# Last piece of the down projection as two 256-column halves in banks of their own, its sum of squares on DVE, final scaling split 384 to 640

## The chip, the cores and the metric

The kernel runs on one core of a Trainium2 chip. The metric is the device time in microseconds (us). The engines are TensorE (PE, with its weight load PEld), VectorE (DVE), ScalarE (ACT), GpSimd (POOL) and SyncE (SP), which issues most of the DMA.

## The reference, cut to what matters

Two layers, each with an attention mixer and a gated MLP with a causal depthwise convolution, both with a norm in front and a residual add behind; at the end one more RMS norm. The sequence has 256 positions, the model 1024 columns, the MLP 2816.

```python
def rmsnorm(x, g):
    xf = x.astype(jnp.float32)
    y = xf * lax.rsqrt(jnp.mean(xf * xf, axis=-1, keepdims=True) + NORM_EPS)
    return (y * g.astype(jnp.float32)).astype(x.dtype)

def conv_glu_ffn(h, w_up, conv_w, conv_b, w_down):
    a, u = jnp.split(h @ w_up, 2, axis=-1)
    a = lax.conv_general_dilated(...) + conv_b
    return (jax.nn.silu(a) * u) @ w_down

    for i in range(DEPTH):
        ...
        h = rmsnorm(x, norm2_g[i])
        x = x + conv_glu_ffn(h, w_up[i], conv_w[i], conv_b[i], w_down[i])
    return rmsnorm(x, final_g)
```

## The kernel before, in words

The residual stream stays on the chip as `xr`, 128 partitions by two tiles of positions (t = 0, 1) by 1024 columns. fp32 products are made of three matmuls each (`mm3`, L206 to L208: high by high, high by low, low by high), so each weight tile `st` that arrives by DMA is split into a high part `hl` on ACT (L158) and a low part on DVE (L160).

The MLP of a layer goes over NF = 11 blocks of 256 hidden columns. `up(f)` makes 256-column matmuls (L919 to L921) into two banks of role u0 or u1, by f odd or even, then the convolution and the gate on DVE and ACT, and ends in `h_hi` and `h_lo`. `down(fs, which)` adds the down projection of the blocks fs into the banks `dn[n, t]`, where n is the half of 512 output columns and t the tile of positions; in the traces these four banks are called bn. Within the loop, `down` of block f - 1 follows `up(f)` on TensorE. The last two blocks (9 and 10) come after the loop. In the last layer they come piece by piece, in the order (n, t) = (0, 0), (1, 0), (0, 1), (1, 1), 12 matmuls of 512 columns a piece. Behind each piece, `add` (L962) puts the bank and `xr` together on DVE, `sumsq` (L179) squares the 512 columns with a running sum on ACT, and the gain `fg` is multiplied in on POOL for n = 0 and on DVE for n = 1 (L1000).

When both pieces of a tile are there, the mean is put together by POOL (m0, L1002) and DVE (m1, L1003), POOL raises it to the power of -1/2 (L1004), ACT scales the first 512 columns (L1005) and DVE the other 512 (L1007), and the two halves are stored from SP's queue (L1006) and ACT's (L1008). Nothing else is left to do behind the piece (1, 1) of the last layer.

The order of instructions on each engine is made by a scheduler within the framework; each engine runs its own list in order. [...]

## Time and profile before

| | |
|---|---|
| three runs | 661.97, 664.06, 664.2 us; median 664.06 |
| the profiled execution | 662.68 us, span 660.9 us |
| mean granted TensorE clock | 0.997 of full speed |
| busy | PE 97%, PEld 88%, DVE 75%, ACT 57%, POOL 8% |
| chain that ended last | PE 81%, DVE 11%, the rest 2% or less each |

The span runs from the first to the last instruction of the profiled execution; its time is 1.78 us more. A share of busy time is a mean over the whole span. The chain is followed back from the last instruction, at each step to what released it.

### The profile page before, as it was taken

How to read it: one execution, taken by the hardware profiler on the slowest of the kernel's cores; microseconds unless marked ns; L12 is line 12 of the kernel's file. 1: busy time of each engine (PE TensorE's matmuls, PEld its weight loads, DVE VectorE, ACT ScalarE, POOL GpSimd, SP SyncE). 2: the span in 40 equal slices, each digit the busy share in tenths (PEclk: the TensorE clock that was granted, in tenths of full speed). 3: DMA queues.
4: the chain of work that ended last, by engine and by line, in shares of the span. 5: the costliest groups of instructions: out<-in, count | busy, mean ns of one | idle time of the engine just before them, and what ended most of it. 6: DMA issues, size and time to landing. Idle time of an engine off the chain costs nothing.

```text
span 660.9 us, 11729 instructions
## 1 busy us (share of the span) xinstructions
PE 641.7 (97%) x4403; PEld 578.4 (88%) x4403; DVE 497.5 (75%) x1093; ACT 375.5 (57%) x683; POOL 50.3 (8%) x119
## 2 busy tenths in 40 slices
PE   8989999999999999999999999999999999999995
PEld 6978987779999999999898888877999999999994
DVE  5979998776766677777587799986697776666653
ACT  6666667775544444455475676785654455544523
POOL 0522210001000000000020242000000000000002
PEclk9999999999999999999999999999999999999998
DMA  8982423454665565565457525234465655566601
GB/s 268 279 265 72 126 83 113 134 184 158 192 188 185 179 188 184 182 182 160 128 167 228 149 71 176 81 110 155 127 218 189 184 182 182 187 191 190 191 1 63
DMA packets 76535, 107.34 MB, mean 162 GB/s; under 512 B 3717, under 2 KB 63414, under 8 KB 76480
## 3 DMA queue, kind: packets, MB, share of 16 engines
q1 hardware_dynamic: 75568, 104.77, 51.2%
q0 software_dynamic: 448, 1.05, 0.5%
q8 instruction: 34, 0.56, 0.3%
q10 hardware_dynamic: 464, 0.79, 0.3%
q14 instruction: 21, 0.17, 0.1%
HBM read 105.55 MB, written 1.05 MB: 161 GB/s over the span
## 4 chain that ended last, share of the span: by engine, by line
PE 81%; DVE 11%; DMA 2%; issue 2%; ACT 2%; POOL 1%; POOLq 0%; DVEq 0%; ACTq 0%
PE bu L921 13%; PE bu L920 13%; PE bu L919 13%; PE bn L206 6%; PE bn L207 6%; PE bn L208 6%; PE bd L206 5%; PE bd L208 5%; PE bd L207 5%; DVE hl L160 3%; PE bs L352 2%; DMA st<-in_w_in_dram 2%; PE bt L372 2%; PE bt L341 1%; DVE acc L484 1%
## 5 line engine op out<-in xcount | busy, mean ns | idle before, releaser
L160 DVE TENSOR_TENSOR hl<-st,hl 128x1024 fp32r<-128x1024 f32 (+3 forms) x208 | 230.7, 1120 | 97.3 <-ACT hl L158 96.8
L158 ACT CAST hl<-st 128x1024 fp32r<-128x1024 f32 (+3 forms) x208 | 198.0, 970 | 136.4 <-PE bu L921 68.1
L920 PE MATMUL bu<-alo,hl 128*128 128x256 f32 x704 | 199.7, 284 | 1.3 <-DVE alo L196 1.3
L921 PE MATMUL bu<-ahi,hl 128*128 128x256 f32 x704 | 199.0, 283 | 0.0
L919 PE MATMUL bu<-ahi,hl 128*128 128x256 f32 x704 | 197.9, 283 | 0.0
L920 PEld LDWEIGHTS bu<-alo,hl 128*128 128x128 f32 x704 | 135.1, 192 | 2.4 <-DVE alo L196 1.7
L919 PEld LDWEIGHTS bu<-ahi,hl 128*128 128x128 f32 x704 | 134.5, 192 | 1.3 <-ACT ahi L195 0.3
L921 PEld LDWEIGHTS bu<-ahi,hl 128*128 128x128 f32 x704 | 135.1, 192 | 0.0
L206 PE MATMUL bd<-hl,ahi 128*128 128x384 f32 (+2 forms) x256 | 92.9, 367 | 2.3 <-ACT hl L158 1.4
L207 PE MATMUL bd<-hl,ahi 128*128 128x384 f32 (+2 forms) x256 | 91.4, 357 | 0.4 <-DVE hl L160 0.4
L208 PE MATMUL bd<-hl,alo 128*128 128x384 f32 (+2 forms) x256 | 91.2, 356 | 0.0
L206 PE MATMUL bn<-hl,h_hi 128*128 128x512 f32 x176 | 68.9, 392 | 0.0
L207 PE MATMUL bn<-hl,h_hi 128*128 128x512 f32 x176 | 68.6, 391 | 0.0
L208 PE MATMUL bn<-hl,h_lo 128*128 128x512 f32 x176 | 68.4, 390 | 0.0
L206 PEld LDWEIGHTS bd<-hl,ahi 128*128 128x128 f32 x256 | 48.0, 188 | 11.0 <-ACT hl L158 3.0
L207 PEld LDWEIGHTS bd<-hl,ahi 128*128 128x128 f32 x256 | 48.2, 188 | 3.6 <-issue 0.8
L208 PEld LDWEIGHTS bd<-hl,alo 128*128 128x128 f32 x256 | 48.2, 188 | 3.1 <-issue 0.9
L208 PEld LDWEIGHTS bn<-hl,h_lo 128*128 128x128 f32 x176 | 33.0, 188 | 7.4 <-DVE h_lo L943 0.4
L206 PEld LDWEIGHTS bn<-hl,h_hi 128*128 128x128 f32 x176 | 33.1, 188 | 6.6 <-ACT h_hi L942 0.5
L207 PEld LDWEIGHTS bn<-hl,h_hi 128*128 128x128 f32 x176 | 33.1, 188 | 6.0
L931 DVE SCALAR_TENSOR_TENSOR c<-a,colc,c 128x255 f32<-128x255 f32 (+1 forms) x88 | 36.7, 477 | 0.7 <-ACT c L929 0.7
L934 ACT ACTIVATE th<-c 128x512 f32<-128x512 f32 x22 | 13.9, 632 | 35.1 <-DVE c L931 35.1
(242 smaller groups left out, 782.0 us busy)
## 6 DMA issues: line engine op xcount, KB each, us to landing
st<-in_w_up_dram SPq DMA_DIRECT2D x88, 512.0 KB, 3.6
st<-in_w_down_dram SPq DMA_DIRECT2D x44, 512.0 KB, 3.5
st<-in_w_in_dram SPq DMA_DIRECT2D x40, 384.0 KB, 3.8
st<-in_w_out_dram SPq DMA_DIRECT2D x12, 512.0 KB, 3.8
st<-in_w_in_dram SPq DMA_DIRECT2D x8, 360.0 KB, 3.5
st<-in_w_in_dram SPq DMA_DIRECT2D x8, 336.0 KB, 3.6
st<-in_w_out_dram SPq DMA_DIRECT2D x8, 256.0 KB, 3.0
xr<-in_x_dram SPq DMA_DIRECT2D x3, 256.0 KB, 5.9
```

The costliest lines, as they stand in the source:

```text
L158: S.copy(hv, sv)
L160: V.tensor_sub(lv, sv, hv.bitcast(F32))
L206: PE.matmul(b, ahi, whi, start=first, stop=False)
L207: PE.matmul(b, ahi, wlo, start=False, stop=False)
L208: return PE.matmul(b, alo, whi, start=False, stop=last)
L352: PE.matmul(b[:, o:o + nk], qa, ka, start=True, stop=True)
L372: PE.transpose(b[:, j * 128:(j + 1) * 128], P[:, j * 128:(j + 1) * 128], ident)
L919: PE.matmul(o, wa, hhi[k // 4][:, k % 4, :], start=k == 0, stop=False)
L920: PE.matmul(o, wa, hlo[k // 4][:, k % 4, :], start=False, stop=False)
L921: PE.matmul(o, wl, hhi[k // 4][:, k % 4, :], start=False, stop=k == 7)
L931: V.scalar_tensor_tensor(c[:, o + d:o + 256], a[:, o:o + 256 - d], cw[w], c[:, o + d:o + 256], op0=OP.mult, op1=OP.add)
L934: S.activation(th, c, AF.Tanh, scale=0.5)
```

## The change

In the last layer alone:

- The piece (1, 1) of the last two blocks no longer adds into its old bank. That bank's sum ends with block 8 (`f1 = NF - 3`), and `add(1, 1)` takes it into `xr` ahead of the closing loop. The last two blocks make two pieces of 256 columns, each in a bank of role u1 of its own, so the last 12 matmuls of 512 columns become 24 of 256.
- Behind each piece comes an add, a square with a sum into a column of its own, and the gain. For the very last piece the square runs on DVE with an accumulator output (L1011); the others stay on ACT.
- The gain of each tile's last piece is issued on DVE behind the mean instruction (L1017) instead of ahead of it.
- ACT scales 384 columns and DVE 640, and the stores are divided in the same way.

```diff
+                    f1 = NF - 3 if i == DEPTH - 1 and (n, t) == (1, 1) and into is None else NF - 1
...
-                            q, c = slice(t * 128, (t + 1) * 128), slice(n * 512, (n + 1) * 512)
-                            mm3(dn[n, t], h_hi[:, s, q], h_lo[:, s, q], wh[:, 0, c], wl[:, 0, c],
-                                f == 0 and s == 0, f == NF - 1 and s == 1)
+                            q, c = slice(t * 128, (t + 1) * 128), slice(n * 512 + part.start, n * 512 + part.stop)
+                            mm3(dn[n, t] if into is None else into, h_hi[:, s, q], h_lo[:, s, q], wh[:, 0, c], wl[:, 0, c],
+                                f == (0 if into is None else fs[0]) and s == 0, f == f1 and s == 1)
...
+            add(1, 1)
+
             for t in range(2):
-                m0, m1, r = (keep.tile([128, 1], F32, name=f"fin{j}{t}") for j in range(3))
-                y = [mp.tile([128, 512], F32, name=f"y{n}", tag=f"y{n}", bufs=2) for n in range(2)]
-                for n in range(2):
-                    down(fs, [(n, t)])
-                    xs = add(n, t)
-                    sumsq(ssq, t, n)
-                    (V if n else G).tensor_mul(y[n], xs, fg[:, n * 512:(n + 1) * 512])
-                    if n == 0:
-                        G.tensor_scalar(m0, ssq[:, t, 0:1], 1.0 / D, EPS, op0=OP.mult, op1=OP.add)
-                V.scalar_tensor_tensor(m1, ssq[:, t, 1:2], 1.0 / D, m0, op0=OP.mult, op1=OP.add)
-                G.tensor_tensor(r, m1, neghalf[:, 0:1], op=OP.pow)
-                S.activation(y[0], y[0], AF.Copy, scale=r)
-                nc.sync.dma_start(out[0, t * 128:(t + 1) * 128, 0:512], y[0])
-                V.tensor_scalar(y[1], y[1], r, None, op0=OP.mult)
-                nc.scalar.dma_start(out[0, t * 128:(t + 1) * 128, 512:1024], y[1])
+                m = [keep.tile([128, 1], F32, name=f"fin{j}{t}") for j in range(3)]
+                sq = keep.tile([128, 3], F32, name=f"fins{t}")
+                r = keep.tile([128, 1], F32, name=f"finr{t}")
+                y = mp.tile([128, D], F32, name="y", tag="y", bufs=2)
+                pieces = [(0, 0, 512), (1, 0, 512)] if t == 0 else [(0, 0, 512), (1, 0, 256), (1, 256, 512)]
+                for j, (n, a, b) in enumerate(pieces):
+                    last = j == len(pieces) - 1
+                    o = None if b - a == 512 else bank("u1")[:, :b - a]
+                    down(fs, [(n, t)], slice(a, b), o)
+                    xs = add(n, t, slice(a, b), o)
...
+                    if last and t:
+                        V.scalar_tensor_tensor(junk[:, :b - a], xs, 1.0, xs, op0=OP.mult, op1=OP.mult,
+                                               accum_out=sq[:, j:j + 1])
+                    else:
+                        S.activation(junk[:, :b - a], xs, AF.Square, accum_out=sq[:, j:j + 1])
+                    mj = None
+                    if j:
+                        mj = V.scalar_tensor_tensor(m[j], sq[:, j:j + 1], 1.0 / D, m[j - 1], op0=OP.mult, op1=OP.add)
+                    else:
+                        G.tensor_scalar(m[0], sq[:, 0:1], 1.0 / D, EPS, op0=OP.mult, op1=OP.add)
+                    with after(mj.ins if last else None):
+                        (V if j else G).tensor_mul(y[:, c], xs, fg[:, c])
+                G.tensor_tensor(r, m[len(pieces) - 1], neghalf[:, 0:1], op=OP.pow)
+                S.activation(y[:, 0:384], y[:, 0:384], AF.Copy, scale=r)
+                nc.sync.dma_start(out[0, t * 128:(t + 1) * 128, 0:384], y[:, 0:384])
+                V.tensor_scalar(y[:, 384:D], y[:, 384:D], r, None, op0=OP.mult)
+                nc.scalar.dma_start(out[0, t * 128:(t + 1) * 128, 384:D], y[:, 384:D])
```

Three places show what the scheduler makes of it. The first is TensorE's list where the last piece begins, in the changed kernel (the bank of the piece ahead is bn_5469, that of the first half bu_7377):

```order
L208 MATMUL bn_5469<-hl,h_lo 128x512
L206 MATMUL bu_7377<-hl,h_hi 128x256 [waits PE_49]
L207 MATMUL bu_7377<-hl,h_hi 128x256
L208 MATMUL bu_7377<-hl,h_lo 128x256
L206 MATMUL bu_7377<-hl,h_hi 128x256
```

Before, the 12 matmuls that follow bn_5469 write bn_5471 with 512 columns and wait for nothing; now 12 write bu_7377 and 12 more bu_7395, and the first of each has a wait for a count of TensorE itself, one reached when the matmuls of `up(9)` into the same bank were done.

The second place is DVE's list for tile 1, from the add of piece (0, 1) on; fg is the gain, ssq and fins hold the sums of squares, fin is the mean or the power. Before:

```order
L962 TENSOR_TENSOR xr<-bn_5469,xr 128x512 [waits PE_49]
L962 TENSOR_TENSOR xr<-bn_5471,xr 128x512 [waits PE_49]
L1000 TENSOR_TENSOR y_7356<-xr,fg 128x512 [waits DVE_49]
L1003 SCALAR_TENSOR_TENSOR fin_7353<-ssq,fin_7352 128x1 [waits Activation_49,Pool_49]
L1007 TENSOR_SCALAR y_7356<-y_7356,fin_7354 128x512 [waits Pool_49]
```

And in the changed kernel (L964 is the add, L1021 the gain, L1017 the mean, L1011 the square, L1025 the scaling; finr is the power):

```order
L964 TENSOR_TENSOR xr<-bn_5469,xr 128x512 [waits PE_49]
L964 TENSOR_TENSOR xr<-bu_7377,xr 128x256 [waits PE_49]
L1021 TENSOR_TENSOR y<-xr,fg 128x256 [waits DVE_49]
L1017 SCALAR_TENSOR_TENSOR fin_7355<-fins_7357,fin_7354 128x1 [waits Activation_49,Pool_49]
L964 TENSOR_TENSOR xr<-bu_7395,xr 128x256 [waits PE_49]
L1011 SCALAR_TENSOR_TENSOR junk,fins_7357<-xr 128x256 [waits DVE_49]
L1017 SCALAR_TENSOR_TENSOR fin_7356<-fins_7357,fin_7355 128x1 [waits DVE_49]
L1021 TENSOR_TENSOR y<-xr,fg 128x256
L1025 TENSOR_SCALAR y<-y,finr_7358 128x640 [waits DVE_49,Pool_49]
```

Three instructions became two sets for the halves, with a square between the last add and the last mean, and the gain went behind the mean.

The third place is DVE's list between the gate of block 9 (h_lo) and the first vector instruction of block 10 (a), in the changed kernel; hl are the low parts of the last two down weights:

```order
L160 TENSOR_TENSOR hl<-st,hl 128x1024 [waits DMAHW0_49,Activation_49]
L943 TENSOR_TENSOR h_lo<-u,h_hi 128x512 [waits Activation_49]
L964 TENSOR_TENSOR xr<-bn_5471,xr 128x512 [waits PE_49]
L160 TENSOR_TENSOR hl<-st,hl 128x1024 [waits DMAHW1_49,Activation_49]
L160 TENSOR_TENSOR hl<-st,hl 128x1024 [waits DMAHW2_49,Activation_49]
L923 TENSOR_TENSOR a<-bu_7188,R 128x512 [waits PE_49]
```

The add of bn_5471 is new there; before, the two weight splits follow h_lo at once.

## Rows read from the trace of the kernel before

Times of a timeline are the start and the duration in us; "idle before" is how long the engine had waited and for whom.

**Rows 1.** The page: the span, busy time, share and instructions of the engines, and the shares of the chain that ended last.

```profile
span 660.9 us, 11729 instructions
...
PE 641.7 (97%) x4403; PEld 578.4 (88%) x4403; DVE 497.5 (75%) x1093; ACT 375.5 (57%) x683; POOL 50.3 (8%) x119
...
PE 81%; DVE 11%; DMA 2%; issue 2%; ACT 2%; POOL 1%; POOLq 0%; DVEq 0%; ACTq 0%
```

**Rows 2.** The timeline: the first and the last of 24 matmuls of 256 columns of `up(10)`, which follow each other at equal steps, the DVE instruction that waits for the last of them, and the first and the last of the 12 matmuls of piece (1, 1).

```profile
640.04 0.28 PE L919 MATMUL bu<-ahi,hl 128*128 128x256 f32 x1
...
642.80 0.28 PE L921 MATMUL bu<-ahi,hl 128*128 128x256 f32 x1
...
643.12 0.69 DVE L937 SCALAR_TENSOR_TENSOR u<-bu,R 128x512 f32<-128x512 f32 x1 [1.02 <-PE bu L921]
...
651.33 0.39 PE L206 MATMUL bn<-hl,h_hi 128*128 128x512 f32 x1
...
653.82 0.39 PE L208 MATMUL bn<-hl,h_lo 128*128 128x512 f32 x1
```

**Rows 3.** The timeline behind the last matmul, all engines and the two queues that issue the stores.

```profile
654.25 0.69 DVE L962 TENSOR_TENSOR xr<-bn,xr 128x512 f32<-128x512 f32 x1 [1.89 <-PE bn L208]
654.98 0.69 DVE L1000 TENSOR_TENSOR y<-xr,fg 128x512 f32<-128x512 f32 x1
655.03 0.63 ACT L179 ACTIVATE junk<-xr 128x512 bf16<-128x512 f32 x1 [1.86 <-DVE xr L962]
655.57 0.19 ACT L179 ACTIVATION_READ_ACCUMULATOR junk<-xr 128x1 f32 x1
655.86 0.16 DVE L1003 SCALAR_TENSOR_TENSOR fin<-ssq,fin 128x1 f32<-128x1 f32 x1 [0.19 <-ACT junk L179]
656.11 0.55 POOL L1004 TENSOR_TENSOR fin<-fin,neghalf 128x1 f32<-128x1 f32 x1 [2.10 <-DVE fin L1003]
656.69 0.72 ACT L1005 ACTIVATE y<-y,fin 128x512 f32<-128x512 f32 x1 [0.94 <-POOL fin L1004]
656.69 0.49 DVE L1007 TENSOR_SCALAR y<-y,fin 128x512 f32<-128x512 f32 x1 [0.67 <-POOL fin L1004]
657.21 0.35 ACTq L1008 DMA_DIRECT2D out_dram<-y  x1
657.44 0.34 SPq L1006 DMA_DIRECT2D out_dram<-y  x1
```

**Rows 4.** The timeline where tile 0's scaling ends and the first piece of tile 1 is added.

```profile
651.28 0.49 DVE L1007 TENSOR_SCALAR y<-y,fin 128x512 f32<-128x512 f32 x1 [0.69 <-POOL fin L1004]
...
651.68 0.68 DVE L962 TENSOR_TENSOR xr<-bn,xr 128x512 f32<-128x512 f32 x1
...
652.44 1.29 POOL L1000 TENSOR_TENSOR y<-xr,fg 128x512 f32<-128x512 f32 x1 [1.20 <-DVE xr L962]
...
653.82 0.19 POOL L1002 TENSOR_SCALAR fin<-ssq 128x1 f32<-128x1 f32 x1
```

**Rows 5.** Groups of instructions by line and shape over the whole span, first DVE, then ACT: line, engine, operation, tiles, shapes and count, then busy us and mean ns of one, then idle time before.

```profile
L931 DVE SCALAR_TENSOR_TENSOR c<-a,colc,c 128x255 f32<-128x255 f32 x44 | 19.3, 477 | 0.7 <-ACT c L929 0.7
...
L763 DVE TENSOR_SCALAR P<-P,recs 128x256 f32<-128x256 f32 x20 | 6.1, 347 | 0.0
...
L962 DVE TENSOR_TENSOR xr<-bn,xr 128x512 f32<-128x512 f32 x8 | 5.5, 688 | 7.2 <-PE bn L208 7.2
...
L367 DVE TENSOR_TENSOR ksw<-bt,ksw 128x256 fp32r<-128x256 f32 x4 | 1.7, 421 | 0.1
...
L258 DVE SCALAR_TENSOR_TENSOR junkv<-xr 128x512 bf16<-128x512 f32 x2 | 1.4, 687 | 0.0
...
L1007 DVE TENSOR_SCALAR y<-y,fin 128x512 f32<-128x512 f32 x2 | 1.0, 487 | 1.4 <-POOL fin L1004 1.4
...
L258 DVE DVE_READ_ACCUMULATOR junkv<-xr 128x1 f32 x2 | 0.2, 82 | 0.0
...
L858 ACT ACTIVATE Pd<-Pd,facd 128x256 f32<-128x256 f32 x12 | 5.2, 500 | 1.6 <-DVE facd L850 1.6
...
L1005 ACT ACTIVATE y<-y,fin 128x512 f32<-128x512 f32 x2 | 1.4, 723 | 1.9 <-POOL fin L1004 1.9
```

**Rows 6.** The timeline around the last step of the loop: the first matmul of `down` of block 8, the last matmul of that `down`, DVE's splits of the last two down weights, the first vector instruction of block 10, and the weight load of TensorE that waits for its h_hi.

```profile
625.94 0.40 PE L206 MATMUL bn<-hl,h_hi 128*128 128x512 f32 x1
...
631.18 0.39 PE L208 MATMUL bn<-hl,h_lo 128*128 128x512 f32 x1
...
632.01 2.36 DVE L160 TENSOR_TENSOR hl<-st,hl 128x1024 fp32r<-128x1024 f32 x2 [1.71 <-ACT hl L158]
637.36 0.69 DVE L923 TENSOR_TENSOR a<-bu,R 128x512 f32<-128x512 f32 x1 [2.99 <-PE bu L921]
...
645.24 0.19 PEld L206 LDWEIGHTS bn<-hl,h_hi 128*128 128x128 f32 x1 [0.29 <-ACT h_hi L942]
```

**Rows 7.** DMA from 655 to 661 us: share of 16 engines in tenths and GB/s, both in 40 equal slices, and the two stores with their time from issue to landing.

```profile
DMA  0000000000000000000039999999950000000000
GB/s 0 0 0 0 0 0 0 0 0 0 0 0 0 0 0 0 0 0 0 0 137 410 396 410 355 383 382 410 382 219 14 0 0 0 0 0 0 0 0 0
...
out_dram<-y ACTq DMA_DIRECT2D x1, 256.0 KB, 2.0
out_dram<-y SPq DMA_DIRECT2D x1, 256.0 KB, 2.5
```

More of the change, by code (lines that the diff above doesn't have):

```diff
@@ L948, in trunk, with down @@
                     dn[n, t] = bank(f"n{n}")
-            def down(fs, which):
+            def down(fs, which, part=slice(0, 512), into=None):
                 for n, t in which:
+                    f1 = NF - 3 if i == DEPTH - 1 and (n, t) == (1, 1) and into is None else NF - 1
                     for f in fs:
@@ L955, in down, with add @@
                             wh, wl = wd[s]
-                            q, c = slice(t * 128, (t + 1) * 128), slice(n * 512, (n + 1) * 512)
-                            mm3(dn[n, t], h_hi[:, s, q], h_lo[:, s, q], wh[:, 0, c], wl[:, 0, c],
-                                f == 0 and s == 0, f == NF - 1 and s == 1)
-            def add(n, t):
-                xs = xr[:, t, n * 512:(n + 1) * 512]
-                V.tensor_tensor(xs, dn[n, t], xs, op=OP.add)
+                            q, c = slice(t * 128, (t + 1) * 128), slice(n * 512 + part.start, n * 512 + part.stop)
+                            mm3(dn[n, t] if into is None else into, h_hi[:, s, q], h_lo[:, s, q], wh[:, 0, c], wl[:, 0, c],
+                                f == (0 if into is None else fs[0]) and s == 0, f == f1 and s == 1)
+            def add(n, t, part=slice(0, 512), b=None):
+                xs = xr[:, t, n * 512 + part.start:n * 512 + part.stop]
+                V.tensor_tensor(xs, dn[n, t] if b is None else b, xs, op=OP.add)
                 return xs
@@ new lines, in trunk @@
+                sq = keep.tile([128, 3], F32, name=f"fins{t}")
[7 more added lines that the diff above has]
+                    xs = add(n, t, slice(a, b), o)
+                    c = slice(n * 512 + a, n * 512 + b)
+                    junk = keep.tile([128, 512], BF, name="junk", tag="junk", bufs=1)
+                    if last and t:
[10 more added lines that the diff above has]
+                        (V if j else G).tensor_mul(y[:, c], xs, fg[:, c])
```

## The prediction

> **What bounds the kernel now.** I read the head of the page first: TensorE is busy for 97% of the span, and 81% of the chain that ended last is TensorE [rows 1]. So only two kinds of edit can matter: one that changes TensorE's work or makes it wait, and one in the tail behind its last matmul, where it has nothing left to do. Then I read the timeline of the last 20 us, in the order in which the chain of waits runs through it. The last matmul of the down projection starts at 653.82 [rows 2]. Behind it comes a pure chain [rows 3]: add on DVE (654.25), square with its sum on ACT (655.03) and the read of the sum (655.57), mean on DVE (655.86), power on POOL (656.11), scaling on ACT and DVE together (656.69), issue of the stores (657.21 on ACT's queue, 657.44 on SP's). The store landing last does so at 657.44 + 2.5 = 659.94 [rows 7], and about 1 us of closing barriers ends the span at 660.9. From the last matmul's start to the end are 7.1 us, 1.1% of the span. That is all the ground that this change has, beside one DVE instruction that it puts earlier.
>
> **The change part by part.** I follow the chain of rows 3 and replace its links.
>
> *The piece in halves.* Before, 12 matmuls of 512 columns start between 651.33 and 653.82, so 2.49/11 = 0.226 us apart. After, 24 of 256 columns. The trace has no 256-column matmul of the down projection, but those of the up projection have the same tile and run unhindered: 23 steps from 640.04 to 642.80, 0.120 us each [rows 2]. The last of 24 then starts 23 x 0.120 = 2.76 us behind 651.33, at 654.09, 0.27 later. From the last matmul's start to the DVE instruction that waits for it is 0.43 us with 512 columns (653.82 to 654.25) and 0.32 with 256 (642.80 to 643.12) [rows 2, 3], which gives back 0.11. **Term: +0.16 us**; the second half's add starts at 654.41. [...] Above: a weight load of a 128x128 tile takes 0.19 us [rows 6]; were the halves paced by it, the term would be far larger (first rival). I take 0.120, because the up projection loads a weight for each matmul too and keeps that pace.
>
> [...]
>
> *The waits for the u1 banks* in front of each half are for matmuls of the up step before the last, done before the down step that starts at 625.94 [rows 6], 25 us earlier: nothing. [...]
>
> *The early add of bank (1, 1).* It is one more DVE instruction of 0.69 us [rows 5]. It waits for the matmul that starts at 631.18 and so runs from about 631.6 to 632.3. Queued behind it on DVE are the two splits of the last down weights, which before start at 632.01, when ACT's copy has come [rows 6]: they move by about 0.3 us. Their user is TensorE at 645.24, and DVE itself then idles until 637.36 [rows 6]. Cost nothing; its cover is that DVE idle time of about 3 us. Without it, 0.7 us would reach the vector work of the last up step.
>
> *Add and sum of squares of the last half.* Before: 654.25 to 655.86, 1.61 us for add, hop to ACT, square, accumulator read, hop back [rows 3]. After, all on DVE with 256 columns. An add of a PSUM tile takes 688 ns at 512 columns and a subtraction 421 ns at 256 [rows 5]; started behind each other they keep some 0.04 us (0.73 from start to start for 0.69 of work) [rows 3]. So 0.46 us. The square with accumulation on DVE is in the trace at 512 columns: 687 ns and 82 ns for the read [rows 5]; at 256 it loses the same 0.27, so 0.42 + 0.08 with about no gap: 0.50. Sum 0.96. **Term: -0.65 us** (between -0.5, if both 256-column instructions take the 0.477 of the convolution's rows and another hop comes in, and -0.7). Mean and power are unchanged: 655.86 to 656.69, 0.83 us. The scaling starts at 656.69 + 0.16 - 0.65 = 656.20. The last half's multiplication by the gain stands behind the mean on DVE (0.42 us from about 655.5) and is over by then, hidden by POOL's power.
>
> *384 to 640.* ACT took 723 ns for 512 columns and 500 for 256 of such a scaling, so about 612 for 384; DVE 487 for 512 and 347 for 256, so 0.55 ns a column and 557 for 640 [rows 5]. Issues follow 0.03 us behind: ACT's queue at 656.20 + 0.59 = 656.79 (**-0.42**), SP's at 656.84 (**-0.60**).
>
> *The stores.* Together still 512 KB; the data move from about 658.0 to 659.5 at close to 400 GB/s, both queues at once [rows 7]. If that stream sets the end, the first issue counts (-0.42), if the last landing does, the second (-0.60). ACT's queue now carries 128 KB more than the other: at the full rate those take 0.3 us within the stream; if one queue alone ran at half the rate, 0.3 us more, and the gain would be about -0.1.
>
> *Tile 0* (t = 0). The gain's multiplication now stands behind the mean on DVE, and the scaling is 640 wide: it starts at 651.3 as before and ends 0.07 to 0.11 later, so the add that starts at 651.68 [rows 4] slips by 0.1, and with it POOL's multiplication and its mean term: from 653.82 + 0.19 = 654.01 to about 654.1. DVE's mean of the first half waits for that and for ACT's square of the first half (add at 652.97, square, read, hop: about 654.2). It ends at about 654.4, just when the second half's add wants DVE (654.41). Cost 0 to 0.1, in the sum 0.
>
> **Sum:** -0.5 us (the two issue times bound it at -0.42 and -0.60; with the other ends -0.1 to -0.7). The profiled execution took 662.68 us with a span of 660.9: span 660.4 and 662.2 us afterwards. The median of the three runs is 664.06, 1.4 above the profiled one, so **663.6 us**.
>
> **The rivals.**
>
> *Slower: the halves run at the pace of the weight load.* 24 x 0.19 = 4.56 us instead of 2.72, so the last matmul's start moves by about 1.9 - 0.1 us and the sum is -0.5 - 0.16 + 1.8 = +1.1 us: 665.2. It decides once a 256-column matmul takes over 0.120 + 0.5/24 = 0.141 us. For it: there are twice as many loads, and the h tiles differ from the up projection's operands. Against: 0.120 us held over 24 loads and matmuls with the same 128x128 tile [rows 2]. [...] Chance 4%.
>
> *No gain: the first half gets in the way on DVE.* Add, multiplication and mean of the first half must fit between the halves, 1.44 us. If the mean is late (POOL's 1.29 us multiplication, ACT's read) the last add waits in DVE's order. Each 0.1 us costs 0.1; at 0.5 late the change is worth nothing: 664.1. For it: I have only hundredths of a us of room. Against: both its sources were early enough in the rows above. [...] Chance 11%.
>
> *The stores hide it:* the 640-column store decides, and the end moves by 0.1 us: 664.0. For it: unequal queues. Against: both shared 16 engines at 90% and more [rows 7]. Chance 12%.
>
> *A gain or loss of over 0.5%:* that is 3.3 us, about what a measurement of this kernel can tell from no change. The tail is 7.1 us and I touch 3.6 of it. Only the scatter of the runs (661.97 to 664.2 for one kernel) comes near it. Chance 7%.
>
> **How the numbers follow.** Forecast 66%; rivals 4, 11, 12 and 7%. The first four lie within 0.5% of before; the last 7, scatter between runs or something outside the tail, I divide: faster 0.04, same 0.93, slower 0.03. The costs alone give 663.4 to 665.2; the scatter of the median is larger: 661.97 - 0.7 = 661.3 at the low end, 664.2 + 0.5 (half of the slower rival) = 664.7 at the high end.
>
> **What would show it.** After: 24 matmuls in the last piece 0.120 us apart; the last add some 0.16 later than 654.25; ACT out of the chain behind it; square to mean within 0.55 us; the scaling's two halves ending within 0.1 us of each other; stores issued 0.4 to 0.6 us earlier in a span that is else equal up to 651 us. Wrong it would be with matmuls over 0.14 us apart, with DVE idle before the last add on POOL or ACT, with ACT's store landing over 0.3 us behind SP's, or with a new wait of TensorE near 645.

## The result and the profile after

The changed kernel takes 660.24 us in the median (659.98 to 660.55), the one before 663.84 us on the same chip (661.97 to 664.2), six runs each: ratio 0.995, 95% interval 0.9937 to 0.9963. Its profiled execution took 660.13 us. The prediction was 663.6 us with a range from 661.3 to 664.7, so it was wrong: the gain is 3.6 us where 0.5 was forecast, and below the range. It also lies outside the place that the prediction looked at. One run of the kernel before took 1034.82 us at a granted clock of 0.556; it is of a slow state and is left out of every number here.

The page of the changed kernel, the lines that answer to [rows 1]:

```profile
span 658.4 us, 11760 instructions
...
PE 641.8 (97%) x4415; PEld 579.2 (88%) x4415; DVE 499.6 (76%) x1099; ACT 374.8 (57%) x683; POOL 50.8 (8%) x119
...
PEclk9999999999999999999999999999999999999998
...
PE 85%; DVE 10%; ACT 2%; issue 2%; POOL 1%; POOLq 0%; DVEq 0%; ACTq 0%
```

The busy times are as before; the span is 2.5 us shorter, and the chain has lost the 2% that it spent on DMA (that row proves little alone: when the same kernel ran again, e15 below, its chain had DMA 2% once more). PEclk, the clock granted to TensorE in 40 slices of the span, in tenths of full speed, is as before. Where the 2.5 us lie, busy time by stretch shows. First the kernel before, then the changed one, the first 50 us and the rest (columns: stretch, its length, busy us and instructions of PE, PEld, DVE, ACT and POOL, granted clock, DMA share, GB/s):

```profile
0.00:50.00 50.00, 43.02 (x314) 38.61 (x314) 37.12 (x92) 31.83 (x60) 14.12 (x33) 1.00 0.86 269
50.00:660.90 610.90, 598.67 (x4091) 539.74 (x4089) 460.35 (x1002) 343.67 (x623) 36.16 (x86) 1.00 0.50 154
```

```profile
0.00:50.00 50.00, 45.55 (x329) 41.09 (x330) 39.53 (x99) 33.47 (x63) 14.02 (x33) 1.00 0.85 277
50.00:658.40 608.40, 596.28 (x4087) 538.14 (x4086) 460.07 (x1001) 341.31 (x620) 36.81 (x86) 1.00 0.50 154
```

TensorE gets 2.5 us more work done in the first 50 us, in which the change alters no instruction; nothing is gained behind them. TensorE waits there for weights, with DMA at 86% of its time (85% after). The last of these waits ends with the first matmul on the compression weights `w1` (`cmp_w1`, loaded at L603 into a buffer of role hl, 1 MB a tile in rows of 512 bytes; the profile names the tile w). Timeline from the last matmul ahead of it, before and then after:

```profile
37.25 0.33 PE L208 MATMUL bd<-hl,alo 128*128 128x360 f32 x1
39.71 0.54 PE L607 MATMUL bo<-w,raw 128*32 128x128 f32 x12 [2.13 <-issue]
```

```profile
36.05 0.33 PE L208 MATMUL bd<-hl,alo 128*128 128x360 f32 x1
37.19 1.95 PE L607 MATMUL bo<-w,raw 128*32 128x128 f32 x64 [0.81 <-issue]
```

From there to the end are 621.2 us in both (660.90 - 39.71, 658.36 - 37.19). So the whole difference of these two executions lies in front of w1, and the tail, with all that was changed there, is worth nothing. Of the 2.5 us, 1.32 were saved between the two matmuls shown (2.46 us apart before, 1.14 after), and 1.20 ahead of them. What comes late there is not w1 itself, whose second load has landed by 34.7 us (32.3 after), but the load of st that is issued behind it and takes 9.7 us to land (8.6 after): ACT's split of that tile starts at 35.84 us, after 2.52 of waiting for DMA (33.32 and 1.23 after), 3.87 us ahead of the first matmul on w1 in both.

The tail of the changed kernel, to be laid beside [rows 2 to 4]; all engines but for most matmuls:

```profile
647.97 0.69 DVE L1021 TENSOR_TENSOR y<-xr,fg 128x512 f32<-128x512 f32 x1
...
648.11 0.99 POOL L1022 TENSOR_TENSOR finr<-fin,neghalf 128x1 f32<-128x1 f32 x1 [1.12 <-DVE fin L1017]
...
648.77 0.28 PE L206 MATMUL bu<-hl,h_hi 128*128 128x256 f32 x1
...
649.13 0.55 DVE L1025 TENSOR_SCALAR y<-y,finr 128x640 f32<-128x640 f32 x1 [0.47 <-POOL finr L1022]
...
649.60 0.68 DVE L964 TENSOR_TENSOR xr<-bn,xr 128x512 f32<-128x512 f32 x1
...
650.36 1.31 POOL L1021 TENSOR_TENSOR y<-xr,fg 128x512 f32<-128x512 f32 x1 [1.27 <-DVE xr L964]
...
650.40 0.42 DVE L964 TENSOR_TENSOR xr<-bu,xr 128x256 f32<-128x256 f32 x1
...
650.86 1.09 DVE L1021 TENSOR_TENSOR y<-xr,fg 128x256 f32<-128x256 f32 x1
...
651.52 0.28 PE L208 MATMUL bu<-hl,h_lo 128*128 128x256 f32 x1
651.76 0.25 POOL L1019 TENSOR_SCALAR fin<-fins 128x1 f32<-128x1 f32 x1
652.04 0.16 DVE L1017 SCALAR_TENSOR_TENSOR fin<-fins,fin 128x1 f32<-128x1 f32 x1
652.12 0.42 DVE L964 TENSOR_TENSOR xr<-bu,xr 128x256 f32<-128x256 f32 x1
652.57 0.42 DVE L1011 SCALAR_TENSOR_TENSOR junk<-xr 128x256 bf16<-128x256 f32 x1
652.92 0.08 DVE L1011 DVE_READ_ACCUMULATOR junk<-xr 128x1 f32 x1
653.03 0.16 DVE L1017 SCALAR_TENSOR_TENSOR fin<-fins,fin 128x1 f32<-128x1 f32 x1
653.11 0.42 DVE L1021 TENSOR_TENSOR y<-xr,fg 128x256 f32<-128x256 f32 x1
653.28 0.66 POOL L1022 TENSOR_TENSOR finr<-fin,neghalf 128x1 f32<-128x1 f32 x1 [1.27 <-DVE fin L1017]
653.97 0.62 ACT L1023 ACTIVATE y<-y,finr 128x384 f32<-128x384 f32 x1 [2.33 <-POOL finr L1022]
653.97 0.55 DVE L1025 TENSOR_SCALAR y<-y,finr 128x640 f32<-128x640 f32 x1 [0.45 <-POOL finr L1022]
654.56 0.37 ACTq L1026 DMA_DIRECT2D out_dram<-y  x1
654.61 0.34 SPq L1024 DMA_DIRECT2D out_dram<-y  x1
```

And the stores, KB and us from issue to landing, which answer to [rows 7]:

```profile
out_dram<-y ACTq DMA_DIRECT2D x1, 320.0 KB, 2.6
out_dram<-y SPq DMA_DIRECT2D x1, 192.0 KB, 2.7
```

From the first matmul of the last piece to the end are 9.57 us before (651.33 to 660.90) and 9.59 us after (648.77 to 658.36). The page rounds the changed kernel's span up to 658.4, so that the expectations below say 9.63 where the trace has 9.59, and 3.84 for the 3.80 of the last link. Link by link:

| link | before | forecast | after |
|---|---|---|---|
| first to last matmul of the piece | 2.49 | 2.76 | 2.75 |
| last matmul's start to last add | 0.43 | 0.32 | 0.60 |
| last add to power | 1.86 | 1.21 | 1.16 |
| power to scaling | 0.58 | 0.58 | 0.69 |
| scaling to first issue (ACT's queue) | 0.52 | 0.59 | 0.59 |
| first issue to the end | 3.69 | 3.69 | 3.80 |

DVE's multiplication by the gain at 650.86, 256 columns wide, takes 1.09 us instead of the 0.42 that the same form takes at 653.11. It ends at 651.95, 0.28 behind POOL's multiplication. POOL's mean term stands behind that multiplication (651.76), DVE's mean behind both (652.04), and the last add behind the mean (652.12).

That mean term is late because tile 0 is. Tile 0's gain multiplication now stands behind its mean (647.97) and so runs beside POOL's power, which takes 0.99 us (648.11). Before, the multiplication came first, and the power of tile 0 took 0.57:

```profile
650.67 0.57 POOL L1004 TENSOR_TENSOR fin<-fin,neghalf 128x1 f32<-128x1 f32 x1 [1.11 <-DVE fin L1003]
```

Counted from the first matmul of the last piece, tile 0's scaling starts at 0.36 us instead of -0.05, the add of tile 1's first piece at 0.83 instead of 0.35, POOL's multiplication at 1.59 instead of 1.11, and its mean term at 2.99 instead of 2.49 [rows 4]. DVE's own multiplication of 1.09 us is over (651.95) before that term is (652.01), so it delays nothing here.

### The profile page after: what moved, and what is told of

Same layout as the page of the kernel before. It is cut to its first block, busy times and chain, and to the rows that moved or that the text cites. A ratio compares the mean times of both kernels' runs of the same rounds, so it can differ in the third digit from the quotient of the medians.

```text
span 658.4 us, 11760 instructions
## 1 busy us (share of the span) xinstructions
PE 641.8 (97%) x4415; PEld 579.2 (88%) x4415; DVE 499.6 (76%) x1099; ACT 374.8 (57%) x683; POOL 50.8 (8%) x119
## 4 chain that ended last, share of the span: by engine, by line
PE 85%; DVE 10%; ACT 2%; issue 2%; POOL 1%; POOLq 0%; DVEq 0%; ACTq 0%
PE bu L920 13%; PE bu L921 13%; PE bu L919 13%; PE bn L206 6%; PE bn L207 6%; PE bn L208 6%; PE bd L206 6%; PE bd L207 5%; PE bd L208 5%; DVE hl L160 3%; PE bs L352 2%; PE bt L372 2%; PE bt L341 1%; DVE acc L484 1%; ACT hl L158 1%
## 5 line engine op out<-in xcount | busy, mean ns | idle before, releaser
L206 PE MATMUL bn<-hl,h_hi 128*128 128x512 f32 x172 | 67.3, 392 | 0.0
L207 PE MATMUL bn<-hl,h_hi 128*128 128x512 f32 x172 | 67.0, 391 | 0.0
L208 PE MATMUL bn<-hl,h_lo 128*128 128x512 f32 x172 | 66.8, 389 | 0.0
L208 PEld LDWEIGHTS bn<-hl,h_lo 128*128 128x128 f32 x172 | 32.3, 188 | 7.2 <-DVE h_lo L943 0.4
L206 PEld LDWEIGHTS bn<-hl,h_hi 128*128 128x128 f32 x172 | 32.4, 188 | 6.6 <-ACT h_hi L942 0.5
L207 PEld LDWEIGHTS bn<-hl,h_hi 128*128 128x128 f32 x172 | 32.4, 188 | 5.8
```

The source lines that it names most:

```text
L206: PE.matmul(b, ahi, whi, start=first, stop=False)
L207: PE.matmul(b, ahi, wlo, start=False, stop=False)
L208: return PE.matmul(b, alo, whi, start=False, stop=last)
```

## The experiments

**What moved in front of w1.** No instruction there differs, but addresses do: the four new small tiles (`sq` and `r` for each t) lie in the pool that lasts, and in the compiled program all that is allocated behind them begins 128 bytes a partition further on. st goes from byte 34,176 to 34,304 (133.5 and 134 times 256), the hl buffers, w1 in them, from 87,424 to 87,552 (341.5 and 342 times 256), and the work tiles likewise. So the theory was: transfers into tiles 128 bytes past a multiple of 256 are slower. The rival was scatter, or the instructions of the tail. The first two runs move the addresses alone, in either kernel, by a small tile that nothing uses, behind the kernel's own small tiles and ahead of st:

```diff
+            keep.tile([128, 32], F32, name="pad")
```

> The kernel before with 128 unused bytes a partition at the end of its lasting pool, and nothing else. All that is allocated behind it moves up by 128 bytes, as it does in the changed kernel: the weight tiles st begin at 34304 instead of 34176 (a multiple of 512 bytes, before 384 past one). Theory 'placement': the first 50 us get 2 to 3 us shorter as in the changed kernel, the time falls by 2.5 to 3.6 us to 660.3 to 661.3. Theory 'tail': the time stays at 663.8 plus or minus 0.4, since no instruction changed.

> The changed kernel with 128 unused bytes more at the end of its lasting pool: the tail is that of the change, the weight tiles st begin at 34432, 128 past a multiple of 256 bytes (as far off a multiple of 256 as before). Theory 'placement': the gain is gone, 663.4 to 664.0, with the same tail as the changed kernel. Theory 'tail': 660.2 as the changed kernel.

Measured: the kernel before with the pad takes 660.79 us against 663.05 without (0.9961, 0.9947 to 0.9975), the changed kernel with it 663.15 us (1.0, 0.999 to 1.0011). A pad that computes nothing gives the gain to the one and takes it from the other. The address is the cause, the instructions of the tail aren't.

**Which tile.** A pad between st and the hl buffers, one in front of st, or both shift parts apart. e3 sets st alone at a multiple of 256 (in the kernel before), e4 all behind st but not st, e5 (the changed kernel) moves the hl buffers with w1 off it and sets the rest behind them right again:

```diff
+    between = []
...
+        if not between:                                       # ahead of the first hl buffer
+            between.append(wst.tile([128, 32], F32, name="pad2"))
...
+            keep.tile([128, 32], F32, name="pad")             # e3 only, ahead of st
+            wst.tile([128, 32], F32, name="pad3")             # e5 only, behind the hl buffers
```

> The kernel before with st alone on a multiple of 512 bytes: 128 bytes of padding ahead of st, 128 more between st and hl, so that hl, the operands of TensorE and all work tiles lie 128 past a multiple of 256 as before. If the place at which the weight DMA writes is the cause: as e1, 660.3 to 661.3. If it is the place from which the engines read (hl, ahi, alo): 663.8.

> The complement of e3: the kernel before with 128 bytes of padding between st and hl alone. st stays where it was, hl, ahi, alo and the work tiles lie as in the changed kernel. If the place at which the weight DMA writes is the cause: 663.8 plus or minus 0.4. If the engines' operands are: 660.3 to 661.3.

> The changed kernel with 128 bytes between st and hl and 128 more behind hl: the hl buffers, among them those that hold the compression weights w1, lie 128 past a multiple of 256 as in the kernel before; st, ahi, alo and the work tiles lie on multiples of 256 as in the changed kernel. Theory 'w1': the 2048-byte packets of the w1 loads take 114 ns again instead of 91, the first matmul that reads w1 starts 2 to 3 us later, time 662.5 to 663.4. Theory 'operands' (ahi, alo or work tiles): 660.2 as the changed kernel.

Measured: e3 662.46 us (0.999, 0.998 to 1.0001), e4 660.37 (0.9959, 0.9946 to 0.9973), e5 661.89 against 663.72 before (0.9979, 0.9969 to 0.999). st at its multiple isn't needed (e4) and does not do it alone (e3). e4 came out on the side of 'the engines' operands', e3 between the two. But the hl buffers hold w1 too, which DMA writes directly, and that is what the next runs take apart. With w1 off, part of the gain is lost (e5), but less than was expected (662.5 at least).

**The row length of w1.** If a row of 512 bytes pays for its place, one long row should pay little (an assumption). e6 is the kernel before with w1 loaded as one row of 8,192 bytes a partition, at the old address; each partition then holds other rows of these weights than its products want, so that part of the output is changed:

```diff
-                    nc.sync.dma_start(w1, cmp_w1[i, c].rearrange("(j p) h -> p j h", p=128))
+                    nc.sync.dma_start(w1, cmp_w1[i, c].rearrange("(p j) h -> p j h", p=128))
```

> The kernel before, all addresses as they were, but w1 is read with 16 neighbouring rows of the weight to a partition: 8192 bytes in one piece instead of 16 pieces of 512 bytes (the compression branch then multiplies by permuted weights, so this leaves out the right order of w1; the amount of work is the same). Theory 'w1 in short rows': its loads get faster than 8.6 us from first to last packet although the place is unaligned, the wait in front of the first matmul on w1 shrinks, 660 to 661. Theory 'w1's place whatever the rows': 663.1.

Measured: 660.76 us (0.9962, 0.995 to 0.9975), first matmul on w1 at 37.7. The full gain, without moving a byte of any buffer, so that the addresses from which the engines read can't be its cause.

**w1's place by itself.** e9 and e10 differ in nothing but where w1's rows begin in their buffer (0 and 32 floats); for the room, 15 of the 16 row groups are loaded:

```diff
-                    w1 = wst.tile([128, 16, 128], F32, name="w1", tag="hl", bufs=NHL)
-                    nc.sync.dma_start(w1, cmp_w1[i, c].rearrange("(j p) h -> p j h", p=128))
+                    w1 = wst.tile([128, 2048], F32, name="w1", tag="hl", bufs=NHL)[:, 32:32 + 1920]
+                    w1 = w1.rearrange("p (j h) -> p j h", j=15)
+                    nc.sync.dma_start(w1, cmp_w1[i, c, 0:1920].rearrange("(j p) h -> p j h", p=128))
```

> The changed kernel with 15 of the 16 row groups of each tile of compression weights loaded (the last group is left out, and the fourteenth stands in for it in the products), so that the tile can be put anywhere in its buffer. Here it begins where the buffer begins, a multiple of 256 bytes. Theory 'place of w1': packets of 2048 bytes between 20 and 45 us last 89 to 95 ns in the mean, the first matmul on w1 starts at 36.9 to 38.0 us, time 659.5 to 660.9 us. Rival 'the work tiles or the state behind the gains, not w1': the same numbers here, and again in the next run.

> The same kernel as the run before in every instruction, transfer and allocation, but for w1's 15 row groups beginning 128 bytes further into their buffer (the 16th group is left out there too). Theory 'place of w1': packets of 2048 bytes back to 112 to 116 ns, first matmul on w1 at 38.8 to 40.0 us, time 661.7 to 663.3 us, 1.5 to 3 us above the run before. Rival 'not w1': within 0.5 us of the run before, 2048-byte packets 89 to 95 ns.

Measured: 661.16 us and 662.26 us (0.9967, 0.9955 to 0.9979, and 0.9983, 0.9974 to 0.9993), 1.1 us apart, less than the 1.5 that the theory wanted at least, more than the rival's 0.5; e9 itself lies 0.3 us above its range. The first matmul on w1 and the landing of the loads into these tiles, at 0 and then at 128 bytes:

```profile
L608 PE MATMUL bo<-w,raw x128: 269/273/297, 36.9 to 361.0; 128*32 128x128 f32 x128
...
DMA to landing us min/median/max: 3.9/6.4/9.7
```

```profile
L608 PE MATMUL bo<-w,raw x128: 270/273/297, 38.6 to 362.7; 128*32 128x128 f32 x128
...
DMA to landing us min/median/max: 3.5/6.7/11.4
```

36.9 and 38.6 us, and the slowest load lands after 9.7 and 11.4 us. From the last matmul ahead of w1 to the first on it are 1.06 and 2.20 us, 1.1 apart as the times are. The packets of the trace say the same for all kernels (those of e9 and e10 are of 512 bytes, not of 2,048 as was expected). These are the packets of w1's size between 20 and 48 us of each profiled execution, worked out from the trace's list of packets: their mean, their sum divided by 16 engines, and the time of all other packets up to then, also by 16:

```
kernel               w1 past 256  packets        mean ns   w1 us   others us
before               128          1040 x 2048 B   114.0     7.41    22.78
e2, e3, e5           128          1040 x 2048 B   113-115   7.35-7.47  22.5-23.0
e10                  128          3856 x  512 B    31.7     7.64    22.90
after                0            1040 x 2048 B    90.6     5.89    22.67
e1, e4, e7, e8, e11 to e15   0    1040 x 2048 B    91-95    5.9-6.2  22.4-23.2
e9                   0            3856 x  512 B    27.1     6.53    22.59
e6 (long rows)       128          257 x 8192 B    354.1     5.69    22.37
```

Where w1 lies 128 bytes past a multiple of 256, its rows of 512 bytes take a quarter longer (114.0 against 90.6 ns for four of them; in e10 and e9 a sixth, 31.7 against 27.1 ns for one), and its two tiles 1.2 to 1.6 us more of the DMA engines' time, 1.1 us for the shortened tiles of e9 and e10, just what their times differ by. All other packets take the same, 22.4 to 23.2 us in every kernel. Why such a row takes longer no run shows. st's rows of 1,536 bytes don't: the median of their packets is 65 ns in the kernel before, with st 128 bytes past a multiple of 256, and 65 ns in the changed one, with st at a multiple.

**Is it st after all?** e13 puts st alone 128 bytes off in the changed kernel (the pads of e3, `pad` and `pad2`, both), and e15 is the changed kernel again beside it.

> The changed kernel with st alone 128 bytes past a multiple of 256; hl, w1 and the work tiles behind it at a multiple. Theory 'only w1 counts': time and start of the first matmul on w1 as in the changed kernel on the same chip (within 0.5 us; 36.9 to 38.2 us), 2048-byte packets 89 to 95 ns. Rival 'st has a part of about 1 us': first matmul on w1 0.7 to 1.2 us later, time 0.7 to 1.3 us above.

> The changed kernel as it is, the control for the two others of this call. Both theories: 660.0 to 660.9 us, first matmul on w1 at 36.9 to 38.2 us, from the first matmul of the last piece to the end 9.55 to 9.7 us.

Measured: 661.14 and 660.93 us (0.9963, 0.9951 to 0.9975, and 0.9957, 0.9944 to 0.997), no difference. Both profiled executions were the slowest of their runs and began w1 at 38.9, later than expected; so one execution places this start to about 2 us only, and the times and the packets decide. The runs with both st and w1 off lie 2.3 to 3.6 us above those with w1 in place (before against e1 and the changed kernel, e2 against the changed kernel), and w1's packets account for 1.2 to 1.6 of that.

Two more numbers bear on the rest. The first is the wait in front of w1, from the start of the last matmul ahead of it: 2.1 to 3.0 us in the five traces with w1's short rows off, 0.9 to 2.1 in the twelve others. That last matmul itself starts anywhere from 35.6 to 38.1 us, whatever w1's place, so this start is scatter, and with it the 1.20 us above. The second is the mean granted clock of each run. It is 0.996 of full speed or lower in 72 of the 112 runs with w1's short rows off, and in 4 of the 67 others. The 51 runs of the kernel before at such a clock have a median of 663.72 us, its other 15 runs one of 662.62, and the 63 runs with w1 in place or in long rows at a higher clock one of 660.76. So about 1 us of the gain goes with the clock, and about 1.9 us is left at like clocks. In none of the 17 traces, whose own means are 0.997 or more, does PEclk fall ahead of the last slice. So it isn't shown where the clock fell in those runs, nor that the longer wait made it fall.

With w1 off, st in its place seems worth 0.6 us (e3 against before), which is not clear of noise; e5, 1.8 us below before, has the work tiles and the other operands in place as well. With w1 in place st is worth nothing (e4 with 660.37 us, e13 with 661.14 against 660.93 in e15). Why was not found.

**Does any other tile count?** e8 moves the residual, the identity and the constants to a multiple too, with the mean's order of e7:

```diff
+            keep.tile([128, 32], F32, name="pad0")      # ahead of xr
```

> e7 with 128 bytes of padding ahead of everything and 128 more at the end of the lasting pool, so that also xr, the identity and the constants lie on multiples of 256 bytes (before, and in the changed kernel, 128 past one); st and hl move from multiples of 512 to 256 past one. If only loads in 512-byte rows feel their place: as e7 within 0.3 us. If each load does: the first loads (xr, constants) come earlier and the time falls by 0.5 us or more. If 512 rather than 256 is the step that matters: the gain of the placement is lost, 662.5 to 663.

Measured: 661.05 us, as e7's 661.21. st and the hl buffers then lie at odd multiples of 256 and w1's packets take 91 to 95 ns as in the other kernels with w1 in place, so a multiple of 256 was enough here and one of 512 isn't needed, and the places of xr, the identity and the constants are worth nothing.

**The tail: who makes the last add late.** The reading of the rows above was POOL's order: the mean term behind the long multiplication. e7 puts it ahead:

```diff
-                        G.tensor_scalar(m[0], sq[:, 0:1], 1.0 / D, EPS, op0=OP.mult, op1=OP.add)
-                    with after(mj.ins if last else None):
+                        mj = G.tensor_scalar(m[0], sq[:, 0:1], 1.0 / D, EPS, op0=OP.mult, op1=OP.add)
+                    with after(mj.ins if last or not j else None):
```

> The changed kernel with POOL's mean term of the first piece issued ahead of its 1.3 us multiplication by the gain, for both tiles. If the last add waited for that term in DVE's order: it starts 3.07 us behind the first matmul of the halves instead of 3.35, DVE's multiplication of the first half no longer runs beside POOL's and takes 0.42 us instead of 1.09, the span is 0.2 to 0.35 us shorter, time about 660.0. If something else held the add: no change, 660.2 to 660.4.

Measured: 661.21 us, and a longer tail: the last add starts 1.14 us behind the last matmul's start instead of 0.60. POOL's multiplication, now behind a term that needs ACT's sum, starts 2.70 us behind the first matmul of the last piece instead of 1.59, just ahead of DVE's mean:

```profile
652.08 1.27 POOL L1020 TENSOR_TENSOR y<-xr,fg 128x512 f32<-128x512 f32 x1
652.37 1.00 DVE L1016 SCALAR_TENSOR_TENSOR fin<-fins,fin 128x1 f32<-128x1 f32 x1 [0.46 <-ACT junk L1014]
653.28 0.41 DVE L964 TENSOR_TENSOR xr<-bu,xr 128x256 f32<-128x256 f32 x1
```

DVE's mean, one element a partition, takes 1.00 us instead of 0.16 and ends at 653.37, when POOL's multiplication does (653.35). So the two hold each other up: in both traces the DVE instruction with two inputs in SBUF that starts beside POOL's multiplication ends behind it (651.95 for POOL's 651.67 in the changed kernel, 653.37 for 653.35 here). It goes the other way too: POOL's power takes 0.99 us beside DVE's multiplication (648.11, above) and 0.55 alone [rows 3]. In all three it is the one that started later that takes longer. DVE's add, with one input in PSUM, isn't held by POOL's multiplication from 650.36 on (650.40, 0.42). By what means the two hold each other no run shows.

**The tail without POOL's multiplication.** e11 gives tile 1's first gain multiplication to DVE, frees tile 0's from its place behind the mean, and lets POOL add the first two sums:

```diff
+                    elif t and j == 1:
+                        G.tensor_add(m[0], sq[:, 0:1], sq[:, 1:2])
+                        G.tensor_scalar(m[1], m[0], 1.0 / D, EPS, op0=OP.mult, op1=OP.add)
...
-                    with after(mj.ins if last else None):
-                        (V if j else G).tensor_mul(y[:, c], xs, fg[:, c])
+                    with after(mj.ins if last and t else None):
+                        (V if j or t else G).tensor_mul(y[:, c], xs, fg[:, c])
```

> The changed kernel with three instructions of the tail moved: tile 1's gain multiplication of the early middle piece goes from POOL to DVE, the mean of the first two sums from DVE to POOL, and tile 0's gain multiplication of the second piece no longer waits for the mean. Theory 'DVE waits in the tail for POOL, and the two slow each other down': the last addition starts 0.30 to 0.36 us behind the start of the last matmul (0.60 in the changed kernel), DVE's gain multiplications of the last piece's halves take 0.35 to 0.7 us each, and the first matmul of the last piece to the end takes 9.2 to 9.4 us in place of 9.63; time 659.8 to 660.3 us. Rival 'the instructions moved find new waits': 9.5 to 9.9 us, time 660.1 to 660.9 us.

Measured: 660.48 us; the last add starts 0.32 us behind the last matmul, as the prediction had it, and the gain multiplications take 0.43 and 0.42. But from the first matmul of the last piece to the end are 9.46 us, not 9.2 to 9.4: from the add to the power it now takes 1.31 us instead of 1.16.

```profile
652.67 0.42 DVE L964 TENSOR_TENSOR xr<-bu,xr 128x256 f32<-128x256 f32 x1 [0.45 <-PE bu L208]
652.73 0.19 POOL L1020 TENSOR_SCALAR fin<-fin 128x1 f32<-128x1 f32 x1
653.20 0.42 DVE L1011 SCALAR_TENSOR_TENSOR junk<-xr 128x256 bf16<-128x256 f32 x1
653.55 0.08 DVE L1011 DVE_READ_ACCUMULATOR junk<-xr 128x1 f32 x1
653.74 0.16 DVE L1022 SCALAR_TENSOR_TENSOR fin<-fins,fin 128x1 f32<-128x1 f32 x1
```

The square starts 0.53 us behind the add, 0.45 in the changed kernel, and the mean 0.19 us behind the read of the sum, 0.11 there. POOL's second small instruction stands beside the add, but nothing of POOL's beside the mean; the cause of the two is not shown.

**The division 384 to 640.** e12 is the changed kernel with scaling and stores 512 to 512 again:

```diff
-                S.activation(y[:, 0:384], y[:, 0:384], AF.Copy, scale=r)
+                S.activation(y[:, 0:512], y[:, 0:512], AF.Copy, scale=r)
```

(and likewise for DVE's part and both stores).

> The changed kernel with the last scaling and the stores divided 512 to 512 columns as in the kernel before. Theory 'the new division brings nothing, since what the shorter scaling saves the smaller store gives back': both scalings 0.68 to 0.72 us (DVE's 0.45 to 0.5), from the later issue to the end 3.45 to 3.75 us in place of 3.84, and the first matmul of the last piece to the end 9.5 to 9.75 us against 9.63; time within 0.3 us of the changed kernel. Rival 'the division 384 to 640 is worth its 0.1 us': 9.72 us or more.

Measured: 660.82 us; from the start of the scaling to the end 4.22 us, against 4.39 in the changed kernel. Over all profiled executions it is 4.16 to 4.22 in the seven kernels with 512 to 512 and 4.38 to 4.45 in the ten with 384 to 640: the new division costs 0.2 us. A part of it is seen at once: DVE with 640 columns is done later, so the first store is issued 0.59 us behind the scaling's start instead of 0.52. The second store, issued 0.1 us earlier (0.64 us behind the scaling's start instead of 0.75), gains nothing by it: it lands 2.7 us behind its issue instead of 2.5 [rows 7]. The time can't tell, 0.6 us above the changed kernel's 660.24 and 0.1 below the 660.93 of e15.

From the first matmul of the last piece (649.80) to the end are 9.35 us, less than either theory said, because e12 shortens tile 0's scaling on DVE too:

```profile
650.16 0.49 DVE L1025 TENSOR_SCALAR y<-y,finr 128x512 f32<-128x512 f32 x1 [0.47 <-POOL finr L1022]
...
650.56 0.68 DVE L964 TENSOR_TENSOR xr<-bn,xr 128x512 f32<-128x512 f32 x1
...
651.33 1.30 POOL L1021 TENSOR_TENSOR y<-xr,fg 128x512 f32<-128x512 f32 x1 [1.20 <-DVE xr L964]
...
652.71 0.25 POOL L1019 TENSOR_SCALAR fin<-fins 128x1 f32<-128x1 f32 x1
...
653.07 0.42 DVE L964 TENSOR_TENSOR xr<-bu,xr 128x256 f32<-128x256 f32 x1
```

The add of tile 1's first piece comes at 0.76 us instead of 0.83, POOL's multiplication at 1.53 instead of 1.59, its mean term at 2.91 instead of 2.99, the last add at 3.27 instead of 3.35. So the last add follows the end of tile 0's scaling, link by link.

**Both mended.** e14 is e11 without POOL's adding of sums (POOL makes the first mean term as in the changed kernel) and with 512 to 512.

> The changed kernel with tile 1's gain multiplications all on DVE (POOL is then free for the first mean), tile 0's second gain multiplication not held behind the mean, and the scaling and the stores 512 to 512 as in the kernel before. Theory 'the late mean and the stores are all that ate the gain': last addition 0.30 to 0.36 us behind the start of the last matmul, from it to the power 1.14 to 1.20, power to scaling 0.55 to 0.70, scaling to the end 4.12 to 4.27, and from the first matmul of the last piece to the end 9.05 to 9.25 us against 9.57 before and 9.63 in the changed kernel; time 0.3 to 0.6 us below the changed kernel on the same chip. Rival 'a third cost comes up': 9.35 or more, time within 0.25 us of the changed kernel.

Measured: 660.1 us against 660.93 for the changed kernel on the same chip; 0.9948 of before (0.9935 to 0.9961). From the timeline of its tail:

```profile
650.85 0.42 DVE L964 TENSOR_TENSOR xr<-bu,xr 128x256 f32<-128x256 f32 x1
651.11 0.19 POOL L1019 TENSOR_SCALAR fin<-fins 128x1 f32<-128x1 f32 x1 [2.03 <-ACT junk L1014]
...
651.98 0.16 DVE L1017 SCALAR_TENSOR_TENSOR fin<-fins,fin 128x1 f32<-128x1 f32 x1 [0.25 <-ACT junk L1014]
652.24 0.42 DVE L964 TENSOR_TENSOR xr<-bu,xr 128x256 f32<-128x256 f32 x1
...
653.41 0.66 POOL L1022 TENSOR_TENSOR finr<-fin,neghalf 128x1 f32<-128x1 f32 x1 [2.10 <-DVE fin L1017]
```

The mean (651.98) is over before the last add (652.24), which starts 0.32 us behind the last matmul's start (651.92). From the first matmul of the last piece to the end are 9.15 us, 0.42 less than before and 0.44 less than in the changed kernel. Tile 0's power takes 0.57 us again. How much came from tile 0 and how much from tile 1's multiplication on DVE no run takes apart. This is the fastest kernel of this case, though its lead over the changed one is no larger than what the runs scatter by.

## Why the prediction was wrong

**The step that failed** is the bound on the ground: that the tail's 7.1 us and one DVE instruction are "all the ground that this change has", and that the span is "else equal up to 651 us". The change also allocates, a term that the prediction put at nothing without a word. Its four small tiles moved w1 to a better place, and its loads got quicker (e1, e2, e6, e9, e10; packets of 90.6 ns instead of 114.0). The load of st behind them, for which TensorE's work in the first 40 us waits, took 8.6 us to land instead of 9.7. In the kernel before, moving the buffers (e1, e4) or loading w1 in long rows (e6) is worth 2.3 to 3.0 us. The 3.6 us of the two medians are more than that; when the changed kernel ran again, it lay 3.1 below before (e15). Of the 2.5 us between the two profiled executions, the wait in front of w1 gave 1.3, and the rest lies in a stretch that scatters. The tail by itself gave nothing: with w1 off again, the changed kernel took as long as before (e2).

The timelines read for the prediction begin at 625 us [rows 6], and the rest are sums over the whole span [rows 1, 5]. "DMA 2%" in the chain [rows 1] said that TensorE waits for loads somewhere, but nothing in these rows could tell that an address would move. The 7% for "something outside the tail" was the only place for it, with 4% for faster by over 0.5%. The measured gain of 0.5% lies right at that bound.

**The tail's terms, one by one.**
- *The piece in halves*: right. 23 steps of 0.120 us, the last start 2.75 us behind the first. The rival of the weight load's pace did not come.
- *Start of the last add*: wrong. 0.28 us later than forecast. The rival "the first half gets in the way on DVE", held at 11%, is what happened, by the path that it named, POOL's multiplication and the mean behind it, and its price was in the text (0.1 for each 0.1 late). What made the mean late is a term of the prediction's paragraph on tile 0: its scaling was to start "as before" and the next add to slip by 0.1 us. The scaling started 0.41 us late, since the gain's multiplication held POOL's power up, and the add slipped by 0.48. By the rows above, with a slip of 0.1 the mean would have been over at about 2.9 us behind the piece's first matmul, before the add could start at 3.07 (an estimate).
- *Add and square on DVE*: right, -0.70 for -0.65.
- *Power unchanged*: 0.69 us to the scaling instead of 0.58, since DVE's gain multiplication, put behind the mean, now runs beside it. The prediction said hidden by the power; it is hidden, but it lengthens it (0.66 us for 0.55).
- *384 to 640*: lost 0.2 us (e12) where 0.1 was to be had. The durations are right (0.62 and 0.55 for 0.612 and 0.557) and so are the issues behind them, but the stores land later. The first issue fits better than the second, as the text's lower bound had it, but the time from there to the end grew too, by 0.11 us (from the second by 0.29). That is the third rival, the stores, at a part of its price.
- *The early add and the u1 banks*: right, no new wait of TensorE; from the first matmul on w1 to the end both kernels take 621.2 us.

Within the tail the forecast of -0.5 us was therefore not off in the links that it replaced, but in those that it took as unchanged or free: tile 0, the power and the stores. e14 mends the first and the last, and its tail is 0.42 us shorter than before.

## What to carry to other kernels

A change that allocates a tile can move the tiles behind it, here by 128 bytes a partition: before a gain far from the edit is believed, give the kernel before a pad of the same size (with it, e1 took 660.79 us instead of 663.05). Where the start waits for loads and some of them have short rows, try the tiles of these at multiples of 256 bytes, or long rows: w1's packets of 2,048 bytes took 90.6 ns at such a place and 114.0 at 128 bytes past it, where those of 8,192 bytes took 354.1 (e6). Before work is laid beside POOL, look whether DVE's instruction there has two inputs in SBUF: such ones took 1.09 us for 0.42 and 1.00 for 0.16 here and ended behind POOL's, POOL's power took 0.99 for 0.55, and what was late in one tile reached the next (0.41 us in tile 0's scaling, 0.48 in the add behind it). Dividing the last work so that two engines end together gained nothing here: 4.39 us from the scaling to the end against 4.22 in e12, in part as the first store went out later for it (0.59 us behind the scaling's start instead of 0.52).

## What the runs showed of the hardware that was not expected

- Rows of 512 bytes written 128 bytes past a multiple of 256 in a partition: 114.0 ns for four (before) against 90.6 (after), 31.7 for one (e10) against 27.1 (e9); rows of 1,536 bytes 65 ns at either place (before, after).
- DVE instructions with two SBUF inputs beside POOL's multiplication: 1.09 us for 0.42 (after), and 1.00 us for 0.16 (e7); POOL's power beside DVE's: 0.99 us (after) for 0.55 (before).
- The second layer loads w1 in the same way (packets of 2,048 bytes 113.5 ns before, 97.9 after, between 330 and 370 us), and nothing comes of it: 621.2 us from the first matmul on w1 to the end in both.
